# Six PSUM tiles in place of three double ones, gate and value evicted one by one, and mixer steps ranked higher

## The chip, the cores and the metric

The kernel runs on one core of a Trainium2 chip. The metric is the device time of one execution in microseconds (us). The engines are named as in the profile: PE is TensorE's matmul stream and PEld its weight loads, DVE is VectorE, ACT is ScalarE, POOL is GpSimd, SP is SyncE, which issues the transfers.

## The reference

Two layers of a streaming encoder for 256 frames of width 1024, all in float32:

```python
for layer in range(2):
    x = half_ffn(x, ffn_norm[layer, 0], w1, w3, w2)      # x + 0.5 * (silu(h w1) * (h w3)) w2, h = rmsnorm(x)
    h = rmsnorm(x, mix_norm[layer])
    x = x + (mixer_gla_rglru(h) if layer == 0 else mixer_hgrn2(h))
    x = half_ffn(x, ffn_norm[layer, 1], w1, w3, w2)
    gate = sigmoid(rmsnorm(x, ple_norm[layer]) @ ple_gate[layer])
    x = x + gate * (p[layer] @ ple_proj[layer])
return rmsnorm(x, final_norm)
```

The feed-forwards are 1024 to 2816 and back. The first mixer has four gated linear-attention heads and a gated linear recurrence (RG-LRU) with a short convolution, the second has eight heads of a gated recurrence with 128 by 128 states. Each head output goes through a norm of its own, is multiplied with silu of a gate, and then through an output projection.

## The kernel before, in words

Activations lie with the features on the partitions: x is 8 tiles of 128 features by 256 frames. The weights are one stream of 128 by 128 blocks in the order of their use. A transfer (`load`, L394) brings 16 blocks into one of three `raw` buffers. For exactness each weight is split in two parts, for eight blocks at a time: ACT copies them to the short form `wh` (L415) and DVE subtracts that to get the rest `wl` (L416); six buffers of each go round. Activations are split the same way. In the feed-forwards a block (`blk`, L453 and L454, in its last step L450 and L451) is one matmul of `wh` with both parts of the activation (512 columns, one whole PSUM bank) and one of `wl` with the first part (256 columns). In the mixers and the embedding a block (`blk3`, L437 to L439) is three matmuls of 256 columns into half a bank; where the frames are to lie on the partitions, `aproj` (L598 to L600) swaps the operands.

Products are summed in PSUM. There are eight banks. Two, `sgl`, are tiles of their own and serve small products. Six are halves of three tiles `duo` (L317 to L341): `bank()` hands them out in turn, and `bank2()` hands out the two halves of one `duo` together.

A feed-forward (`ffn`) has 22 lifts and 8 down projections. A lift makes the gate in one half of a `duo` and the value in the other; when both are complete, `lift` copies the `wl` halves of both by one ACT instruction of 512 columns (L613), adds them by one DVE instruction (L614), multiplies the gate with the norm's factor (L615), takes silu (L616), multiplies (L617) and splits the result (L618, L619). A down projection uses one bank and is evicted by a copy (L645) and an addition (L646), followed by a scaling and the addition to x. The norm's factor comes from a sum of squares by way of a square root on ACT (L563) and a reciprocal on DVE (L565).

In the mixers, `pairs` makes two products in one bank and `gated2` evicts them (L751); the head outputs `po` get a bank each (L956, L1095), and `Heads.norm` reads it twice: first for the squares (L720), whose mean goes through a root (L730) and two reciprocals (L733), and then for the scaling (L734). `gated` multiplies with the gate (L739) and `split` makes the two parts (L744, L745). In mixer1 the forget gates go through softplus straight from PSUM (L1020).

The order of the work on each engine is written by a planner (`Plan`). Every step is added with its engine, an estimated cost and what it reads and writes. The main matmuls keep the order of the stream. Every other step gets a due time, the latest at which PE would not have to wait for it, and at each moment an engine takes the ready step with the earliest due time. The instructions are then written out in that order, and each engine works through its list in turn. Waits between engines are set by the framework, by the tiles that instructions share. The planner itself follows parts of tiles (`Cell`), so it does not know of waits that come from a shared tile.

Of the kernel before, what the change touches and what calls it, by code (L numbers as in the profile page):

```python
# [13 lines left out]
P = 128  # L14
# [33 lines left out]
class Op:  # L48
    __slots__ = ("eng", "cost", "emit", "deps", "succ", "main", "due", "tab", "port", "left", "ready", "start",
                 "end", "seq", "first", "tag", "lag")  # L50

# [8 lines left out]
MARGIN = 350  # L60
HOLD = 25000


# [4 lines left out]
class Plan:  # L68
    def __init__(self):
        self.ops, self.now = [], 0.0  # L70
        self.phase = None

    def add(self, eng, cost, emit, r=(), w=(), main=False, tab=None, port=False, first=None, tag="", lag=0):
        o = Op()
        o.eng, o.cost, o.emit, o.main, o.tab, o.port, o.first, o.tag, o.lag = eng, cost, emit, main, tab, port, first, tag, lag
        o.deps, o.succ, o.seq = {}, [], len(self.ops)
        r, w = list(r), list(w)
# [27 lines left out]
    def order(self):  # L105
# [7 lines left out]
        for o in reversed(ops):  # L113
            d = o.due if o.eng == "PE" and o.main else last + 2000 - o.cost
            for s in o.succ:
                d = min(d, s.due - s.deps[o] - o.cost)
            o.due = d if o.first is None else o.first
        engines = ("PE", "DVE", "ACT", "POOL", "SP", "NONE")
        free = dict.fromkeys(engines, 0.0)
# [5 lines left out]
        for o in ops:  # L125
            if not o.left:
                heapq.heappush(wait[o.eng], (0.0, o.seq, o))

        def at(e):
# [5 lines left out]
        while len(out) < len(ops):  # L135
# [61 lines left out]
            if o.port:  # L197
                port = o.end
            out.append(o)
            for y in o.succ:  # L200
                y.left -= 1
                y.ready = max(y.ready, o.end + y.deps[o])
                if not y.left:
                    t = y.ready
                    if y.eng == "PE" and not y.main:
                        t += MARGIN
                    heapq.heappush(wait[y.eng], (t, y.seq, y))
        self.out = out
# [29 lines left out]
def kernel(  # L238
# [61 lines left out]

    def dve(n, emit, r, w, port=True, tag=""):
        return plan.add("DVE", 150 + 1.05 * n, emit, r, w, port=port, tag=tag)

# [12 lines left out]

    duo = [pp.tile([P, 2, 2, T], F32, name=f"duo{k}", tag=f"duo{k}") for k in range(3)]  # L317
    sgl = [pp.tile([P, 2, T], F32, name=f"sgl{k}", tag=f"sgl{k}") for k in range(2)]
    banks = []
    for k in range(6):  # L320
        b = Buf()
        b.t = duo[k // 2][:, k % 2]
        banks.append(b)
    sbanks = []
    for k in range(2):
        b = Buf()
        b.t = sgl[k]
        sbanks.append(b)
    sbank = Ring(sbanks)
    bi = [0]  # L330

    def bank():
        bi[0] += 1
        return banks[(bi[0] - 1) % 6]

    def bank2():

        bi[0] += bi[0] % 2
        k = bi[0] % 6
        bi[0] += 2  # L340
        return banks[k], banks[k + 1], duo[k // 2]  # L341

# [54 lines left out]
    def sub(i):  # L397
        if i in subs:
            return subs[i]
        ri, k = divmod(i, RB // SB)  # L400
        if ri not in raws:
            if ri < 4:
                load(ri, 0, 2)
                load(ri, 2, 4)
            else:
                load(ri, 0, 4)
        rb, h, l = raws[ri], wh_ring(), wl_ring()
        n = 2 if i < fine else 1
        for e in range(n):
            w = SB * P // n  # L410
            d = slice(e * w, (e + 1) * w)
            s = slice(k * SB * P + e * w, k * SB * P + (e + 1) * w)
            q = rb(2 * k + e) if n == 2 else rb(2 * k, 2 * k + 1)
            keys = (e,) if n == 2 else (0, 1)
            act(w, lambda d=d, s=s: A.copy(h.t[:, d], rb.t[:, s]), q, h(*keys), tag="wh")  # L415
            dve(w, lambda d=d, s=s: V.tensor_tensor(l.t[:, d], rb.t[:, s], h.t[:, d].bitcast(F32), ALU.subtract),  # L416
                q + h(*keys), l(*keys), tag="wl")
        subs[i] = (h, l)
        return subs[i]
# [185 lines left out]
    def ffn(nm, h, nxt, side=None):  # L605
        ph = Phase(f"f{nm}")
        t_ring, s_ring, lo_ring = ph.ring(2, [P, 2, T], "t"), ph.ring(2, [P, T], "s"), ph.ring(2, [P, 2, T], "lo")
        u2 = [ph.buf([P, 2, T], f"u2_{k}", F32R) for k in range(NF)]

        def lift(f, ba, bb, d):  # L610
            lo, t, s = lo_ring(), t_ring(), s_ring()
            ab = ba() + bb()
            act(2 * T, lambda: A.copy(lo.t, d[:, :, 1]), ab, lo(), tag="lo")  # L613
            dve(2 * T, lambda: V.tensor_add(t.t, d[:, :, 0], lo.t), ab + lo(), t(0, 1), port=False, tag="merge")  # L614
            dve(T, lambda: V.tensor_mul(t.t[:, 0], t.t[:, 0], h.r()), t(0) + h.rb(), t(0), tag="tr")  # L615
            act(T, lambda: A.activation(s.t, t.t[:, 0], AF.Silu), t(0), s(), tab="silu", tag="silu")  # L616
            dve(T, lambda: V.tensor_mul(t.t[:, 1], t.t[:, 1], s.t), t(1) + s(), t(1), tag="tb")  # L617
            act(T, lambda: A.copy(u2[f].t[:, 0], t.t[:, 1]), t(1), u2[f]("h"), tag="uh")  # L618
            dve(T, lambda: V.tensor_tensor(u2[f].t[:, 1], t.t[:, 1], u2[f].t[:, 0].bitcast(F32), ALU.subtract),  # L619
                t(1) + u2[f]("h"), u2[f](), tag="ul")  # L620

        wide = [bank2() for _ in range(2)]
        for c in range(NC):
# [7 lines left out]
        for f in range(2, NF):  # L631
            ba, bb, d = bank2()
            for b in (ba, bb):
                for c in range(NC):
                    m, mb = h.chunk(c)
                    blk(b.t, b(), m, mb, c == 0, c == NC - 1)
            lift(f, ba, bb, d)
        if side is not None:
            side(ph)
        def down(j):  # L640
            b = bank()
            for f in range(NF):
                blk(b.t, b(), lambda f=f: u2[f].t, u2[f]("h", 0), f == 0, f == NF - 1)
            lo, t = lo_ring(), pt_ring()
            act(T, lambda: A.copy(lo.t[:, 0], b.t[:, 1]), b(), lo(), tag="lo")  # L645
            dve(T, lambda: V.tensor_add(t.t, b.t[:, 0], lo.t[:, 0]), b() + lo(), t(), port=False, tag="merge")  # L646
            dve(T, lambda: V.scalar_tensor_tensor(t.t, t.t, 0.5, h.r(), op0=ALU.mult, op1=ALU.mult), t() + h.rb(), t(),
# [146 lines left out]
    def mixer0(nm, h, nxt):  # L794
# [153 lines left out]
        for e in range(2):  # L948
            b = bank()
            rows = slice(e * 64, e * 64 + 64)  # L950
# [48 lines left out]
    def mixer1(nm, h, nxt):  # L999
# [10 lines left out]
        def half(hh):  # L1010
# [77 lines left out]
            for k in range(2):  # L1088
                b = bank()

# [27 lines left out]
    for layer, mixer in enumerate((mixer0, mixer1)):  # L1118
        hm = Normed(f"m{layer}", ("mix", layer * NC), cols=True)
        ffn(f"{layer}0", h, hm, decay_terms if layer == 0 else lower_bound_terms)  # L1120
        hf = Normed(f"f{layer}1", ("ffn", (2 * layer + 1) * NC))
        mixer(f"{layer}", hm, hf)
        hl = Normed(f"p{layer}", ("ple", layer * NC))
        embed(layer)
# [182 lines left out]
```

## Time and profile before

| | us |
|---|---|
| median of 3 runs | 1104.5 |
| lowest, highest | 1101.99, 1104.57 |
| the profiled execution, its own time | 1102.52 |
| its span, first to last instruction | 1100.7 |
| PE busy (share of the span) | 1055.4 (96%) |
| DVE busy | 797.1 (72%) |
| ACT busy | 656.5 (60%) |
| POOL busy | 13.0 (1%) |

One execution was recorded. The busy time of PE counts a matmul until its modelled end; matmuls overlap, and a new one can begin while the one before it is still draining. "Idle before" is the time in which an engine did nothing ahead of an instruction, with what released it. The mean granted clock of PE is 0.994 of full speed. The stages follow each other on one time line: the first feed-forward ends near 202 us, mixer0 near 302, the second feed-forward near 494, the first embedding near 523, the third feed-forward near 718, mixer1 near 863, the last feed-forward near 1055, and then come the last embedding and the final norm.

### The profile page before, as it was taken

The numbers are of one execution on the slowest core, as the hardware profiler recorded it, in microseconds if no ns is written. First come the engines' busy times: TensorE is split into PE (matmuls) and PEld (weight loads), VectorE is DVE, ScalarE is ACT, GpSimd is POOL, SyncE is SP. The second block draws the span as 40 slices with busy tenths as digits, with TensorE's granted clock in tenths as the row PEclk, the third lists the DMA queues.
The fourth block names the chain that finished last, engine by engine and source line by source line (L and its number), as shares of the span: only waits on it lengthen the run. The fifth ranks groups of instructions, "written<-read, shape, count | busy, mean of one in ns | idle before, by whom it ended". The sixth has DMA issues, their size and how long they took to land.

```text
span 1100.7 us, 16250 instructions
## 1 busy us (share of the span) xinstructions
PE 1055.4 (96%) x6452; PEld 931.0 (85%) x6452; DVE 797.1 (72%) x1173; ACT 656.5 (60%) x973; POOL 13.0 (1%) x22
## 2 busy tenths in 40 slices
PE   8999999999999999999999999999998999999995
PEld 7888878889988888889888888789898888887885
DVE  7877766668887776668887776686868877775673
ACT  6666544576666565446765554495856655664452
POOL 4000000000000000000000000000000000000000
PEclk9999999999999999999999999999999999999998
DMA  7656654542555555544555554454433555555421
GB/s 269 230 196 229 211 191 153 178 152 78 203 206 183 181 187 187 180 164 150 196 191 188 182 193 165 159 186 153 149 120 118 187 182 180 182 188 188 158 75 38
DMA packets 28776, 190.14 MB, mean 173 GB/s; under 512 B 3323, under 2 KB 4380, under 8 KB 6684
## 3 DMA queue, kind: packets, MB, share of 16 engines
q1 hardware_dynamic: 28268, 188.53, 49.6%
q8 instruction: 50, 0.82, 0.3%
q10 hardware_dynamic: 432, 0.58, 0.2%
q14 instruction: 26, 0.21, 0.1%
HBM read 188.05 MB, written 1.05 MB: 172 GB/s over the span
## 4 chain that ended last, share of the span: by engine, by line
PE 92%; DVE 3%; ACT 2%; issue 1%; POOL 1%; DMA 0%; SPq 0%; DVEq 0%; ACTq 0%; POOLq 0%
PE duo L453 40%; PE duo L454 20%; PE duo L437 6%; PE duo L438 5%; PE duo L439 5%; PE duo L451 4%; PE duo L450 2%; PE duo L598 2%; PE duo L600 1%; PE duo L599 1%; DVE hsd_m L733 1%; PE duo L1095 1%; DVE pt L646 1%; ACT lo_f L645 1%; DMA xs<-in_xT_dram 0%
## 5 line engine op out<-in xcount | busy, mean ns | idle before, releaser
L416 DVE TENSOR_TENSOR wl<-raw,wh 128x1024 fp32r<-128x1024 f32 (+1 forms) x357 | 431.4, 1213 | 133.1 <-ACT wh L415 132.6
L415 ACT CAST wh<-raw 128x1024 fp32r<-128x1024 f32 (+1 forms) x357 | 368.9, 1038 | 197.7 <-PE duo L453 87.8
L453 PE MATMUL duo<-x,wh 128*128 128x512 f32 x1232 | 442.2, 398 | 3.4 <-DVE x L507 1.5
L454 PE MATMUL duo<-x,wl 128*128 128x256 f32 x1232 | 346.0, 281 | 1.6 <-DVE wl L416 1.6
L453 PEld LDWEIGHTS duo<-x,wh 128*128 128x128 f32 x1232 | 231.8, 188 | 53.0 <-ACT wh L415 2.2
L453 PE MATMUL duo<-u_f,wh 128*128 128x512 f32 x672 | 241.7, 398 | 17.7 <-DVE pt L646 9.4
L454 PEld LDWEIGHTS duo<-x,wl 128*128 128x128 f32 x1232 | 232.8, 189 | 9.5 <-DVE wl L416 2.2
L454 PE MATMUL duo<-u_f,wl 128*128 128x256 f32 x672 | 189.7, 282 | 0.0
L453 PEld LDWEIGHTS duo<-u_f,wh 128*128 128x128 f32 x672 | 126.1, 188 | 54.3 <-DVE pt L646 14.5
L437 PE MATMUL duo<-x,wh 128*128 128x256 f32 x496 | 143.6, 290 | 8.6 <-DVE gt L686 2.1
L438 PE MATMUL duo<-x,wh 128*128 128x256 f32 x496 | 141.1, 284 | 2.8 <-DVE x L745 2.8
L439 PE MATMUL duo<-x,wl 128*128 128x256 f32 x496 | 140.9, 284 | 0.0
L454 PEld LDWEIGHTS duo<-u_f,wl 128*128 128x128 f32 x672 | 126.3, 188 | 1.5
L613 ACT COPY lo_f<-duo 128x512 f32<-128x512 f32 x88 | 51.3, 587 | 119.3 <-PE duo L451 118.8
L437 PEld LDWEIGHTS duo<-x,wh 128*128 128x128 f32 x496 | 95.6, 193 | 12.9 <-DVE gt L686 2.9
L614 DVE TENSOR_TENSOR t_f<-duo,lo_f 128x512 f32<-128x512 f32 x88 | 60.5, 691 | 58.8 <-ACT lo_f L613 58.2
L438 PEld LDWEIGHTS duo<-x,wh 128*128 128x128 f32 x496 | 95.6, 193 | 3.4 <-DVE x L745 3.0
L439 PEld LDWEIGHTS duo<-x,wl 128*128 128x128 f32 x496 | 95.8, 193 | 0.0
L451 PE MATMUL duo<-x,wh 128*128 128x512 f32 x176 | 69.4, 398 | 0.0
L450 PE MATMUL duo<-x,wl 128*128 128x256 f32 x176 | 49.7, 282 | 0.0
L616 ACT ACTIVATE s_f<-t_f 128x256 f32<-128x256 f32 x88 | 36.4, 418 | 20.2 <-DVE t_f L615 20.0
L506 ACT ACTIVATE x<-xs,sml 128x256 fp32r<-128x256 f32 x64 | 31.6, 507 | 19.8 <-DVE xs L649 9.8
(210 smaller groups left out, 976.3 us busy)
## 6 DMA issues: line engine op xcount, KB each, us to landing
raw<-in_ws_dram SPq DMA_DIRECT2D x172, 1024.0 KB, 4.9
raw<-in_ws_dram SPq DMA_DIRECT2D x7, 512.0 KB, 8.5
xs<-in_xT_dram SPq DMA_DIRECT2D x3, 256.0 KB, 6.2
raw<-in_ws_dram SPq DMA_DIRECT2D x2, 256.0 KB, 4.7
praw<-in_pT_dram SPq DMA_DIRECT2D x1, 512.0 KB, 5.9
lb_D<-in_lbl_dram SPq DMA_DIRECT2D x1, 512.0 KB, 5.9
lb_A<-in_lbl_dram SPq DMA_DIRECT2D x1, 512.0 KB, 6.9
bd_m<-in_bdiag_dram SPq DMA_DIRECT2D x1, 512.0 KB, 3.6
```

What stands on the lines that cost most here:

```text
L415: act(w, lambda d=d, s=s: A.copy(h.t[:, d], rb.t[:, s]), q, h(*keys), tag="wh")
L416: dve(w, lambda d=d, s=s: V.tensor_tensor(l.t[:, d], rb.t[:, s], h.t[:, d].bitcast(F32), ALU.subtract), q + h(*keys), l(*keys), tag="wl")
L437: M.matmul(o, wh, mt[:, 0], start=first, stop=False)
L438: M.matmul(o, wh, mt[:, 1], start=False, stop=False)
L439: M.matmul(o, wl, mt[:, 0], start=False, stop=last)
L450: M.matmul(o[:, 0], wl, mt[:, 0], start=False, stop=False)
L451: M.matmul(o, wh, mt, start=first, stop=True)
L453: M.matmul(o, wh, mt, start=first, stop=False)
L454: M.matmul(o[:, 0], wl, mt[:, 0], start=False, stop=False)
L613: act(2 * T, lambda: A.copy(lo.t, d[:, :, 1]), ab, lo(), tag="lo")
L614: dve(2 * T, lambda: V.tensor_add(t.t, d[:, :, 0], lo.t), ab + lo(), t(0, 1), port=False, tag="merge")
L616: act(T, lambda: A.activation(s.t, t.t[:, 0], AF.Silu), t(0), s(), tab="silu", tag="silu")
```

## The change

- The three `duo` tiles and two `sgl` tiles become six tiles `bank` and two tiles `sbank` of one bank each. `bank2()` is gone.
- In `lift` the gate and the value each get a copy and an addition of 256 columns of their own (`merged`), and the gate goes on to silu before the value is read. The three rings behind it hold three tiles of 256 columns.
- In the mixers the stream of products uses banks 0 to 3 (`ring_mix`), and the head outputs banks 4 and 5 (`obank`). Elsewhere all six go round (`ring_all`).
- The due time of each step that is added in a mixer is moved 10 us ahead (`EARLY`), except for the weight conversions.
- While DVE is planned to do a long instruction that does not use the port shared with POOL (over 1.5 us, which means a reciprocal), the planner may hand one subtraction `wl` of 1024 columns that is ready to POOL, if it is not due for 3.6 us.

```diff
 HOLD = 25000
+ALT_NS = 2600
+EARLY = 10000
 
...
         self.ops, self.now = [], 0.0
-        self.phase = None
-
-    def add(self, eng, cost, emit, r=(), w=(), main=False, tab=None, port=False, first=None, tag="", lag=0):
+        self.early = 0
+
+    def add(self, eng, cost, emit, r=(), w=(), main=False, tab=None, port=False, first=None, tag="", lag=0, alt=None):
         o = Op()
+        o.alt = alt
         o.eng, o.cost, o.emit, o.main, o.tab, o.port, o.first, o.tag, o.lag = eng, cost, emit, main, tab, port, first, tag, lag
-        o.deps, o.succ, o.seq = {}, [], len(self.ops)
+        o.deps, o.succ, o.seq, o.early = {}, [], len(self.ops), self.early
         r, w = list(r), list(w)
...
             o.due = d if o.first is None else o.first
+        for o in ops:
+            o.due -= o.early
         engines = ("PE", "DVE", "ACT", "POOL", "SP", "NONE")
...
                 port = o.end
+            done(o)
+            if e == "DVE" and not o.port and o.cost > 1500 and free["POOL"] <= s0 and port <= s0:
+
+                fit = [y for y in ready[e] + wait[e] if y[2].alt and y[2].ready <= s0 + 300
+                       and y[2].due - s0 > ALT_NS + 1000]
+                if fit:
+                    x = min(fit, key=lambda y: y[2].due)
+                    for q in (ready[e], wait[e]):
+                        if x in q:
+                            q.remove(x)
+                            heapq.heapify(q)
+                    y = x[2]
+                    y.eng, y.emit = "POOL", y.alt
+                    y.start = max(s0, y.ready + 90)
+                    y.end = y.start + ALT_NS
+                    free["POOL"] = port = y.end
+                    y.end += 60
+                    done(y)
         self.out = out
...
 
-    def dve(n, emit, r, w, port=True, tag=""):
-        return plan.add("DVE", 150 + 1.05 * n, emit, r, w, port=port, tag=tag)
+    def dve(n, emit, r, w, port=True, tag="", alt=None):
+        return plan.add("DVE", 150 + 1.05 * n, emit, r, w, port=port, tag=tag, alt=alt)
 
...
 
-    duo = [pp.tile([P, 2, 2, T], F32, name=f"duo{k}", tag=f"duo{k}") for k in range(3)]
-    sgl = [pp.tile([P, 2, T], F32, name=f"sgl{k}", tag=f"sgl{k}") for k in range(2)]
-    banks = []
-    for k in range(6):
-        b = Buf()
-        b.t = duo[k // 2][:, k % 2]
-        banks.append(b)
-    sbanks = []
-    for k in range(2):
-        b = Buf()
-        b.t = sgl[k]
-        sbanks.append(b)
-    sbank = Ring(sbanks)
-    bi = [0]
+    banks = [common([P, 2, T], f"bank{k}", pool=pp) for k in range(6)]
+    ring_all, ring_mix, obank = Ring(banks), Ring(banks[:4]), Ring(banks[4:])
+    stream = [ring_all]
 
     def bank():
-        bi[0] += 1
-        return banks[(bi[0] - 1) % 6]
-
-    def bank2():
-
-        bi[0] += bi[0] % 2
-        k = bi[0] % 6
-        bi[0] += 2
-        return banks[k], banks[k + 1], duo[k // 2]
+        return stream[0]()
+
+    sbank = Ring([common([P, 2, T], f"sbank{k}", pool=pp) for k in range(2)])
 
...
         rb, h, l = raws[ri], wh_ring(), wl_ring()
+        early, plan.early = plan.early, 0
         n = 2 if i < fine else 1
...
             act(w, lambda d=d, s=s: A.copy(h.t[:, d], rb.t[:, s]), q, h(*keys), tag="wh")
-            dve(w, lambda d=d, s=s: V.tensor_tensor(l.t[:, d], rb.t[:, s], h.t[:, d].bitcast(F32), ALU.subtract),
-                q + h(*keys), l(*keys), tag="wl")
+
+            def low(E, d=d, s=s):
+                E.tensor_tensor(l.t[:, d], rb.t[:, s], h.t[:, d].bitcast(F32), ALU.subtract)
+
+            dve(w, lambda low=low: low(V), q + h(*keys), l(*keys), tag="wl", alt=n == 1 and (lambda low=low: low(G)))
+        plan.early = early
         subs[i] = (h, l)
...
         ph = Phase(f"f{nm}")
-        t_ring, s_ring, lo_ring = ph.ring(2, [P, 2, T], "t"), ph.ring(2, [P, T], "s"), ph.ring(2, [P, 2, T], "lo")
+        t_ring, s_ring, lo_ring = (ph.ring(3, [P, T], n) for n in ("t", "s", "lo"))
         u2 = [ph.buf([P, 2, T], f"u2_{k}", F32R) for k in range(NF)]
 
-        def lift(f, ba, bb, d):
-            lo, t, s = lo_ring(), t_ring(), s_ring()
-            ab = ba() + bb()
-            act(2 * T, lambda: A.copy(lo.t, d[:, :, 1]), ab, lo(), tag="lo")
-            dve(2 * T, lambda: V.tensor_add(t.t, d[:, :, 0], lo.t), ab + lo(), t(0, 1), port=False, tag="merge")
-            dve(T, lambda: V.tensor_mul(t.t[:, 0], t.t[:, 0], h.r()), t(0) + h.rb(), t(0), tag="tr")
-            act(T, lambda: A.activation(s.t, t.t[:, 0], AF.Silu), t(0), s(), tab="silu", tag="silu")
-            dve(T, lambda: V.tensor_mul(t.t[:, 1], t.t[:, 1], s.t), t(1) + s(), t(1), tag="tb")
-            act(T, lambda: A.copy(u2[f].t[:, 0], t.t[:, 1]), t(1), u2[f]("h"), tag="uh")
-            dve(T, lambda: V.tensor_tensor(u2[f].t[:, 1], t.t[:, 1], u2[f].t[:, 0].bitcast(F32), ALU.subtract),
-                t(1) + u2[f]("h"), u2[f](), tag="ul")
-
-        wide = [bank2() for _ in range(2)]
+        def merged(b, d):
+
+            lo = lo_ring()
+            act(T, lambda: A.copy(lo.t, b.t[:, 1]), b(), lo(), tag="lo")
+            dve(T, lambda: V.tensor_add(d.t, b.t[:, 0], lo.t), b() + lo(), d(), port=False, tag="merge")
+
+        def lift(f, ba, bb):
+            s, t = s_ring(), t_ring()
+            merged(ba, s)
+            dve(T, lambda: V.tensor_mul(s.t, s.t, h.r()), s() + h.rb(), s(), tag="tr")
+            act(T, lambda: A.activation(s.t, s.t, AF.Silu), s(), s(), tab="silu", tag="silu")
+            merged(bb, t)
+            dve(T, lambda: V.tensor_mul(t.t, t.t, s.t), t() + s(), t(), tag="tb")
+            split(lambda: t.t, t(), u2[f])
+
+        wide = [[bank() for _ in range(2)] for _ in range(2)]
         for c in range(NC):
...
         for f in range(2, NF):
-            ba, bb, d = bank2()
-            for b in (ba, bb):
+            ab = [bank() for _ in range(2)]
+            for b in ab:
                 for c in range(NC):
                     m, mb = h.chunk(c)
                     blk(b.t, b(), m, mb, c == 0, c == NC - 1)
-            lift(f, ba, bb, d)
+            lift(f, *ab)
         if side is not None:
             side(ph)
         def down(j):
             b = bank()
             for f in range(NF):
                 blk(b.t, b(), lambda f=f: u2[f].t, u2[f]("h", 0), f == 0, f == NF - 1)
-            lo, t = lo_ring(), pt_ring()
-            act(T, lambda: A.copy(lo.t[:, 0], b.t[:, 1]), b(), lo(), tag="lo")
-            dve(T, lambda: V.tensor_add(t.t, b.t[:, 0], lo.t[:, 0]), b() + lo(), t(), port=False, tag="merge")
+            t = pt_ring()
+            merged(b, t)
             dve(T, lambda: V.scalar_tensor_tensor(t.t, t.t, 0.5, h.r(), op0=ALU.mult, op1=ALU.mult), t() + h.rb(), t(),
...
         for e in range(2):
-            b = bank()
+            b = obank()
             rows = slice(e * 64, e * 64 + 64)
...
             for k in range(2):
-                b = bank()
+                b = obank()
 
...
         hf = Normed(f"f{layer}1", ("ffn", (2 * layer + 1) * NC))
+        stream[0], plan.early = ring_mix, EARLY
         mixer(f"{layer}", hm, hf)
+        stream[0], plan.early = ring_all, 0
         hl = Normed(f"p{layer}", ("ple", layer * NC))
```

## Rows read from the trace of the kernel before

**Rows 1.** The chain that ended last, shares of the span by engine.

```profile
PE 92%; DVE 3%; ACT 2%; issue 1%; POOL 1%; DMA 0%; SPq 0%; DVEq 0%; ACTq 0%; POOLq 0%
```

**Rows 2.** Groups of instructions: busy us, mean ns; idle before, releasers.

```profile
L453 PE MATMUL duo<-u_f,wh 128*128 128x512 f32 x672 | 241.7, 398 | 17.7 <-DVE pt L646 9.4 <-ACT lo_f L645 8.3
...
L437 PE MATMUL duo<-x,wh 128*128 128x256 f32 x496 | 143.6, 290 | 8.6 <-DVE gt L686 2.1 <-DVE xs L656 2.1 <-DVE qs_m L751 1.6
```

**Rows 3.** PE's waits: what it waited for, total us, times, longest us.

```profile
PE duo L453 <- DVE pt L646: 9.4, 16, 0.6
PE duo L453 <- ACT lo_f L645: 8.3, 16, 0.5
PE duo L438 <- DVE x L745: 2.8, 1, 2.8
PE duo L437 <- DVE gt L686: 2.1, 4, 0.5
...
PE duo L453 <- DVE t_f L614: 1.5, 1, 1.5
```

**Rows 4.** Timeline, first feed-forward, 141.5 to 144.7: start us, length us.

```profile
141.53 0.28 PE L450 MATMUL duo<-u_f,wl 128*128 128x256 f32 x1
141.65 0.40 PE L451 MATMUL duo<-u_f,wh 128*128 128x512 f32 x1
141.89 0.39 PE L453 MATMUL duo<-u_f,wh 128*128 128x512 f32 x1
142.12 0.28 PE L454 MATMUL duo<-u_f,wl 128*128 128x256 f32 x1
...
142.50 0.37 ACT L645 COPY lo_f<-duo 128x256 f32<-128x256 f32 x1 [1.58 <-PE duo L454]
142.92 0.50 PE L453 MATMUL duo<-u_f,wh 128*128 128x512 f32 x1 [0.52 <-ACT lo_f L645]
...
143.65 0.42 DVE L646 TENSOR_TENSOR pt<-duo,lo_f 128x256 f32<-128x256 f32 x1 [1.47 <-PE duo L454]
...
144.12 0.50 PE L453 MATMUL duo<-u_f,wh 128*128 128x512 f32 x1 [0.59 <-DVE pt L646]
...
144.58 0.40 PE L453 MATMUL duo<-u_f,wh 128*128 128x512 f32 x1
```

**Rows 5.** Groups of instructions, shapes apart: the evictions of the feed-forwards.

```profile
L614 DVE TENSOR_TENSOR t_f<-duo,lo_f 128x512 f32<-128x512 f32 x88 | 60.5, 691 | 58.8 <-ACT lo_f L613 58.2
L613 ACT COPY lo_f<-duo 128x512 f32<-128x512 f32 x88 | 51.3, 587 | 119.3 <-PE duo L451 118.8 <-DVE t_f L614 0.5
...
L646 DVE TENSOR_TENSOR pt<-duo,lo_f 128x256 f32<-128x256 f32 x32 | 13.5, 423 | 27.0 <-PE duo L454 22.9 <-ACT lo_f L645 4.1
...
L645 ACT COPY lo_f<-duo 128x256 f32<-128x256 f32 x32 | 11.9, 372 | 25.8 <-PE duo L454 16.3 <-PE duo L451 9.5
```

**Rows 6.** Stretches: length, busy PE, PEld, DVE, ACT, POOL, granted clock, DMA, GB/s.

```profile
17.00:134.00 117.00, 117.00 (x666) 101.71 (x666) 94.12 (x138) 74.91 (x115) 0.60 (x2) 1.00 0.63 217
722.00:740.00 18.00, 18.00 (x85) 15.03 (x84) 15.96 (x20) 17.38 (x20) 0.00 (x0) 1.00 0.52 174
842.00:843.00 1.00, 1.00 (x7) 1.00 (x6) 1.00 (x3) 0.00 (x0) 0.00 (x0) 0.50 0.06 25
```

**Rows 7.** Timeline of ACT in mixer1, first half.

```profile
745.89 1.26 ACT L1020 ACTIVATE e_m<-duo,r 128x512 f32<-128x512 f32 x2
```

**Rows 8.** Timeline of DVE at the end of mixer1.

```profile
837.89 3.36 DVE L733 RECIPROCAL hsd_m<-hsd_m 128x256 f32<-128x256 f32 x2 [0.64 <-ACT hsd_m L730]
```

**Rows 9.** Waits of SP's transfer queue, longest.

```profile
SPq L394 <- DVE wl L416: 479.0, 78, 16.6
```

**Rows 10.** Groups of instructions, shapes apart: POOL, and DVE's narrow subtractions.

```profile
L416 DVE TENSOR_TENSOR wl<-raw,wh 128x512 fp32r<-128x512 f32 x10 | 9.3, 943 | 0.5 <-ACT wh L415 0.4
...
L527 POOL TENSOR_TENSOR acc<-acc,sq 128x256 f32<-128x256 f32 x7 | 6.9, 981 | 0.5
...
L520 POOL TENSOR_TENSOR acc<-xs 128x256 f32<-128x256 f32 x1 | 0.6, 613 | 2.8 <-DMA xs<-in_xT_dram 2.8
```

More of the change, by code (lines that the diff above doesn't have):

```diff
@@ L49 @@
     __slots__ = ("eng", "cost", "emit", "deps", "succ", "main", "due", "tab", "port", "left", "ready", "start",
-                 "end", "seq", "first", "tag", "lag")
+                 "end", "seq", "first", "tag", "lag", "early",
+                 "alt")
 LAT = {("PE", "DVE"): 190, ("PE", "ACT"): 220, ("ACT", "DVE"): 45, ("DVE", "ACT"): 60, ("DVE", "PE"): 100,
@@ L127, in order, with done @@
                 heapq.heappush(wait[o.eng], (0.0, o.seq, o))
+        def done(o):
+            out.append(o)
+            for y in o.succ:
+                y.left -= 1
+                y.ready = max(y.ready, o.end + y.deps[o])
+                if not y.left:
+                    t = y.ready
+                    if y.eng == "PE" and not y.main:
+                        t += MARGIN
+                    heapq.heappush(wait[y.eng], (t, y.seq, y))
         def at(e):
@@ L198, in order @@
                 port = o.end
[L199 to L207, printed above, removed]
+            done(o)
[15 more added lines that the diff above has]
+                    done(y)
         self.out = out
```

## The prediction

> **What bounds the kernel now.** I read the chain of waits first: 92% of what ended last is PE [rows 1], so only a change of PE's own work or of the stretches in which PE stands still can move the time. The change leaves every main matmul as it is; so I went to PE's idle time. In the groups of instructions two stand out: 17.7 us before the first matmuls of the down projections (L453 on u_f) and 8.6 us before those of the narrower blocks (L437 on x) [rows 2]. PE's list of waits splits the 17.7 us into 16 waits for the copy of L645 and 16 for the addition of L646, the two steps that evict a finished bank; the 8.6 us are 15 waits for an eviction too, four of them for the gate (L686) [rows 3].
>
> The timeline shows why an eviction holds PE up [rows 4]. The bank of one down projection is complete with the matmul at 141.65 (0.40 long). PE begins the next bank with blocks at 141.89 and near 142.2. The copy of the finished bank could start near 142.1, but starts at 142.50, named as waiting for the matmul of 142.12, which writes the *other* bank. PE's next matmul then waits for the copy (142.92), the addition (143.65) waits for that block's end, and the block after it (144.12) waits for the addition. Both banks are halves of one tile `duo`, and each instruction on a `duo` is held against those on its other half. That is a wait for nothing: no number is shared.
>
> **The change part by part.** All sums are against the profiled execution's own 1102.5 us (span 1100.7 and 1.8 around it); the median of the runs, 1104.5, lies 2.0 above it.
>
> *Each bank a tile of its own.* What one crossing costs: blocks that nothing holds follow each other in 0.36 (141.53 to 141.89), so the fourth from 141.89 on is due at 142.97; it comes at 144.58 [rows 4]. 1.61 are lost, of which 0.52 + 0.59 = 1.11 are idle by the record; the other 0.50, a quarter for each wait, are the modelled end of the matmul before and the longer first matmul after it. So a loss is its idle time plus 0.25 a wait: down projections 17.7 + 32 x 0.25 = 25.7, narrower blocks 8.6 + 15 x 0.25 = 12.4. They occur only where one half of a `duo` is read while its partner is written, and with six tiles that can't be. What is late next? The weights: but no wait for a conversion is listed in those places. The true release of a bank could also hold PE, but in the feed-forward six banks go round, so that at least 16 blocks (5.6 us) lie between a bank's end and its next use. I take all of it there: -38.1, and -25.7 as the weaker end, if the narrower ones turn into other waits.
>
> *Gate and value evicted one by one.* 88 copies of 512 columns (587 ns) become 176 of 256 (372), and 88 additions (691) become 176 (423) [rows 5]: 88 x 157 = 13.8 us more on ACT, 88 x 155 = 13.6 us more on DVE. In the first lift stage ACT is busy 74.9 and DVE 94.1 of 117 us while PE stands still for none of it [rows 6]; 20 lifts add 3.1 to each, so DVE goes from 80% to 83%. Cost on the path nothing, hidden by PE; if that cover fails, 13.6. The rings behind it now hold three feature tiles and not two. The one wait for an addition of L614 (1.5, or 1.8 with its quarter [rows 3]) falls at the start of the third feed-forward, where both slots of t wait for the norm's reciprocal: with a third slot I take it as gone, -1.8 (bounds 0 and -1.8).
> The Trainium skill (Perfetto Trace Analysis, Optimizing Scalar/DVE Operations) says that larger operations pay where the engine is saturated, and that smaller ones can pay where it is not but makes bubbles on others. By its first half this part would cost the 13.6, by its second nothing; the 80% is on the second side.
>
> *Head outputs in two banks, the mixers' stream in four.* Counting the banks handed out, mixer0 starts on banks that were emptied two projections earlier, but mixer1's second bank is that of the very last down projection. It comes free a copy and an addition, 0.37 + 0.42 [rows 4], and three handovers of about 0.1 after its last matmul, 1.1 in all, and PE has three wide matmuls, 0.7, to do before it: 0.4 lost, or 1.6 with a conversion of 1.2 in front; I take 0.5. Second, mixer1's queries now reuse the banks of its forget gates, and the second of these is read by softplus from 745.89 to 747.15 [rows 7] while PE wants it near 746.6; with the first bank's pair a loss of 0 to 2.2, taken as 0.8, since the same change moves softplus forward. That the head outputs leave the stream spares 0.3 of wait at most, which I leave out.
>
> *Mixer steps ranked 10 us higher.* They go ahead of the weight conversions on ACT and DVE. The place that can gain is the end of mixer1: PE waits 2.8 us for the low half of a head output (L745 [rows 3]), which stands on DVE behind two reciprocals, 3.36 [rows 8], and the clock is then granted at half, 0.50 at 842 [rows 6], which on some 15 matmuls of about 0.12 costs 1.4 more. With the quarter of its restart 4.4 in all. If the second head's root is taken before the silu table is loaded, the wait nearly vanishes. Against it, PE arrives there about 1.0 earlier, since one of the 15 waits (0.8 and its quarter) lies just before. Bounds -4.4 and +1.5; I take -1.0, that is -2.0 and the 1.0 given back. The loads inside the mixers carry the higher rank along on SP's queue, but SP spends its time (479 us in that one row) waiting for conversions to free a raw buffer [rows 9], and buffers come free in the order of the loads: nothing.
>
> *Conversions handed to POOL during reciprocals.* At most 20, for 12 head and 8 norm reciprocals. From the 256-column rows, one of 1024 columns is, as an estimate, 4 x 0.61 = 2.5 us with DVE still and 4 x 0.98 = 3.9 beside it [rows 10]; one is chosen only if it is not due for 3.6. DVE gives up 1.2 each time, off the path. So from a gain of 1 to a loss of 20 x (3.9 - 3.6) = 6; I take a loss of 0.5.
> The same page of the Trainium skill warns that the two engines share a port into SBUF, so that such a move might not help. At the kernel's start the trace agrees: 512-column subtractions beside POOL take 943 ns [rows 10], more than the 691 of an addition of that width [rows 5]. By that rule alone DVE gains nothing from the 20, and the sum stays.
>
> Sum: -25.7 - 12.4 - 1.8 - 1.0 + 0.5 + 0.8 + 0.5 = -39.1; 1102.5 - 39.1 = 1063.4, and I say 1063.
>
> **The rivals.**
> *The tail closes too:* mixer1's last wait goes in full and nothing new comes: 1102.5 - 25.7 - 12.4 - 1.8 - 4.4 = 1058. For it: ACT does a weight conversion there, just ahead of the silu table. Against: the chain from the head outputs to the output projection is as long as PE's work beside it.
> *The mixers give part back:* some of the 30 reuses in the ring of four become true waits, an eviction behind a pair of reciprocals coming 3.4 late. Four such are 14 us: 1077. For it: at the start of mixer1 DVE is busy 16.0 and ACT 17.4 of 18 us [rows 6]. Against: between a bank's end and its reuse lie 5 us or more of other PE work.
> *The lifts become bound by DVE:* the 13.6 come on the path, 1077. Against it the 83%.
> *It doesn't do what it says:* an eviction waits for PE's newest matmul whatever the tile; only the 1.8 and the 1.0 go: 1100. Against: the banks of `sgl`, tiles of their own, show no such wait in PE's list.
> *Slower, the conversions starve:* in the mixers a step with 10 us to spare now beats a conversion wanted at once. The place is each burst of mixer work, about six (recurrence and heads of mixer0, gates and heads of both halves of mixer1); the price up to 10 us of PE standing still. It decides from four full bursts, 40 us; six are 60: 1063 + 60 = 1123. For it: ACT's 17.4 of 18. Against: six buffers of eight blocks are 17 us of work ahead, more than the 10.
>
> **How the numbers follow.** Forecast 0.70; tail closes 0.10; mixers give back 0.10; lifts bound 0.04; doesn't do what it says 0.03; starved 0.03. The forecast's own range is 1058 to 1071, its small terms at their bounds. From 1055 to 1077 the range takes in the tail and the edge of the two at 1077, some 0.85 in all. Less than 0.3%, 3.3 us, can't be told from no change. At 1100 the fourth rival is a little under that line below the 1102.5, but over it below the median; I count its 0.03 as same, starvation's 0.03 as slower, the rest, 0.94, as faster.
>
> **What would show it.** In the changed trace: no waits of PE for L645's and L646's like before the down projections, blocks 0.36 apart across their banks; none of 0.5 to 0.8 before the narrow blocks; one of 0.4 to 1 at the start of mixer1; DVE near 83% in the first lift stage with PE full; 176 copies of 0.37 in the lifts; subtractions of 2.5 to 3.9 us on POOL; a gap no longer than before at the end of mixer1. I am wrong if PE waits for conversions inside the mixers, or still stops at every second down projection.

## The result, and the profile after

The changed kernel takes 1057.48 us (median of 4 runs, 1057.01 to 1058.71) against 1103.75 for the kernel before (now four runs; 1104.5 was the median of the first three): a ratio of 0.9585, with a 95% interval of 0.9568 to 0.9601. The profiled execution took 1057.13, 45.4 less than the one before. The page, and PE's waits (the longest, and the two inside mixer1):

```profile
span 1055.1 us, 16450 instructions
...
PE 1041.4 (99%) x6452; PEld 928.8 (88%) x6452; DVE 800.4 (76%) x1259; ACT 651.0 (62%) x1059; POOL 17.8 (2%) x24
...
PE 97%; DVE 1%; POOL 1%; DMA 1%; ACT 0%; issue 0%; SPq 0%; DVEq 0%; ACTq 0%; POOLq 0%
```

```profile
PE sbank L557 <- DVE sq L529: 1.7, 1, 1.7
PE bank L467 <- DVE x L521: 1.4, 2, 1.0
...
PE bank L612 <- DVE pt L628: 0.4, 1, 0.4
...
PE bank L452 <- DVE x L761: 0.3, 1, 0.3
```

The 16 + 16 waits of [rows 3] are gone, and so are the 15 before the narrower blocks; PE's share of the chain goes from 92% [rows 1] to 97%. What is left lies at the kernel's start and end, but for 0.4 at the start of mixer1 and 0.3 at its end. The crossing of [rows 4] now looks so (timeline of the same place: start, length):

```profile
141.61 0.40 PE L465 MATMUL bank<-u_f,wh 128*128 128x512 f32 x1
141.85 0.39 PE L467 MATMUL bank<-u_f,wh 128*128 128x512 f32 x1
142.08 0.28 PE L468 MATMUL bank<-u_f,wl 128*128 128x256 f32 x1
142.10 0.37 ACT L627 COPY lo_f<-bank 128x256 f32<-128x256 f32 x1 [1.23 <-PE bank L465]
...
142.20 0.39 PE L467 MATMUL bank<-u_f,wh 128*128 128x512 f32 x1
...
142.51 0.42 DVE L628 TENSOR_TENSOR pt<-bank,lo_f 128x256 f32<-128x256 f32 x1 [0.38 <-ACT lo_f L627]
...
142.55 0.40 PE L467 MATMUL bank<-u_f,wh 128*128 128x512 f32 x1
```

The copy starts 0.09 after its own bank's last matmul (141.61 + 0.40), names that matmul as its releaser, and PE's blocks follow at 0.35 through it. Copies and additions have become 256 columns wide, at nearly the length of the narrow ones in [rows 5], and the first lift stage answers to [rows 6]:

```profile
L627 ACT COPY lo_f<-bank 128x256 f32<-128x256 f32 x208 | 76.1, 368 | 46.8 <-PE bank L465 46.8
...
L628 DVE TENSOR_TENSOR t_f<-bank,lo_f 128x256 f32<-128x256 f32 x88 | 36.6, 417 | 2.9 <-ACT lo_f L627 2.9
L628 DVE TENSOR_TENSOR s_f<-bank,lo_f 128x256 f32<-128x256 f32 x88 | 36.6, 417 | 3.3 <-ACT lo_f L627 2.9
```

```profile
17.00:134.00 117.00, 117.00 (x666) 101.67 (x665) 95.57 (x161) 75.96 (x138) 0.56 (x2) 1.00 0.63 220
```

PE is full as before, DVE at 82% of it. Where the time went is best seen by stages, from one main matmul's start to the next stage's first (each worked out from the PE timeline of the profiled execution, in us; "down" is the first of four, "lift" the third of four, "embed" the sum of both embeddings, the second up to the first matmul of PE's last group, L1158):

| kernel | median | down | mixer0 | lift | mixer1 | embed |
|---|---|---|---|---|---|---|
| before | 1103.8 | 68.28 | 98.27 | 126.08 | 144.43 | 67.13 |
| after | 1057.5 | 61.82 | 95.30 | 124.33 | 134.60 | 62.37 |
| e1_order | 1077.2 | 61.82 | 96.52 | 127.30 | 146.66 | 65.77 |
| e2_tiles | 1067.9 | 61.82 | 95.48 | 124.33 | 144.33 | 62.36 |
| e3_noearly | 1066.4 | 61.82 | 95.30 | 124.33 | 143.58 | 62.37 |
| e4_allring | 1060.7 | 61.82 | 95.49 | 124.33 | 137.13 | 62.36 |
| e5_duo | 1167.7 | 68.12 | 100.96 | 140.32 | 140.36 | 67.11 |
| e6_noalt | 1060.7 | 61.81 | 95.31 | 124.33 | 138.32 | 62.66 |
| e7_twice | 1058.6 | 61.82 | 96.79 | 124.29 | 134.59 | 62.37 |
| e8_two | 1066.3 | 61.82 | 96.80 | 131.10 | 137.17 | 62.37 |
| e9_early5 | 1059.3 | 61.82 | 96.77 | 124.32 | 136.96 | 62.36 |
| e10_early20 | 1062.3 | 61.81 | 97.45 | 124.33 | 138.17 | 62.36 |
| e11_early40 | 1056.8 | 61.82 | 95.95 | 124.33 | 134.47 | 62.37 |
| e12_offset | 1056.7 | 61.82 | 98.30 | 124.32 | 133.86 | 62.37 |

PE waits for nothing in mixer0 of e7 to e10 and of e12; most of the 1.5 to 3.0 that it is longer there is a stretch in which the clock was granted at half (last section).

### The profile page after: what moved, and what is told of

It reads as the page before. It is cut to its first block, busy times and chain, and to the rows that moved or that the text cites. A ratio compares the mean times of both kernels' runs of the same rounds, so it can differ in the third digit from the quotient of the medians.

```text
span 1055.1 us, 16450 instructions
## 1 busy us (share of the span) xinstructions
PE 1041.4 (99%) x6452; PEld 928.8 (88%) x6452; DVE 800.4 (76%) x1259; ACT 651.0 (62%) x1059; POOL 17.8 (2%) x24
## 4 chain that ended last, share of the span: by engine, by line
PE 97%; DVE 1%; POOL 1%; DMA 1%; ACT 0%; issue 0%; SPq 0%; DVEq 0%; ACTq 0%; POOLq 0%
PE bank L467 41%; PE bank L468 21%; PE bank L451 6%; PE bank L452 6%; PE bank L453 6%; PE bank L465 5%; PE bank L464 2%; PE bank L612 2%; PE bank L614 2%; PE bank L613 2%; PE bank L1111 1%; DMA xs<-in_xT_dram 1%; PE sbank L1086 0%; POOL acc L541 0%; PE sbank L904 0%; PE sbank L1061 0%
## 5 line engine op out<-in xcount | busy, mean ns | idle before, releaser
L467 PE MATMUL bank<-x,wh 128*128 128x512 f32 x1232 | 442.2, 398 | 1.8 <-DVE x L521 1.4
L468 PE MATMUL bank<-x,wl 128*128 128x256 f32 x1232 | 346.0, 281 | 1.4 <-DVE wl L428 1.4
L467 PEld LDWEIGHTS bank<-x,wh 128*128 128x128 f32 x1232 | 231.8, 188 | 51.4 <-ACT wh L425 2.2
L468 PEld LDWEIGHTS bank<-x,wl 128*128 128x128 f32 x1232 | 232.7, 189 | 9.5 <-DVE wl L428 2.3
L467 PE MATMUL bank<-u_f,wh 128*128 128x512 f32 x672 | 237.2, 393 | 0.0
L468 PE MATMUL bank<-u_f,wl 128*128 128x256 f32 x672 | 189.8, 282 | 0.0
L467 PEld LDWEIGHTS bank<-u_f,wh 128*128 128x128 f32 x672 | 126.2, 188 | 27.7
L451 PE MATMUL bank<-x,wh 128*128 128x256 f32 x496 | 141.2, 285 | 0.0
L452 PE MATMUL bank<-x,wh 128*128 128x256 f32 x496 | 140.5, 283 | 0.3 <-DVE x L761 0.3
L453 PE MATMUL bank<-x,wl 128*128 128x256 f32 x496 | 140.3, 283 | 0.0
L468 PEld LDWEIGHTS bank<-u_f,wl 128*128 128x128 f32 x672 | 126.3, 188 | 1.6
L627 ACT COPY lo_f<-bank 128x256 f32<-128x256 f32 x208 | 76.1, 368 | 46.8 <-PE bank L465 46.8
L451 PEld LDWEIGHTS bank<-x,wh 128*128 128x128 f32 x496 | 95.1, 192 | 1.5 <-issue 0.8
L452 PEld LDWEIGHTS bank<-x,wh 128*128 128x128 f32 x496 | 95.1, 192 | 1.1 <-DVE x L761 0.5
L453 PEld LDWEIGHTS bank<-x,wl 128*128 128x128 f32 x496 | 95.1, 192 | 0.0
L465 PE MATMUL bank<-x,wh 128*128 128x512 f32 x176 | 69.5, 398 | 0.0
L464 PE MATMUL bank<-x,wl 128*128 128x256 f32 x176 | 49.7, 282 | 0.0
L464 PEld LDWEIGHTS bank<-x,wl 128*128 128x128 f32 x176 | 33.1, 188 | 8.0
L628 DVE TENSOR_TENSOR s_f<-bank,lo_f 128x256 f32<-128x256 f32 x88 | 36.6, 417 | 3.3 <-ACT lo_f L627 2.9
```

What stands on the lines that cost most here:

```text
L451: M.matmul(o, wh, mt[:, 0], start=first, stop=False)
L452: M.matmul(o, wh, mt[:, 1], start=False, stop=False)
L453: M.matmul(o, wl, mt[:, 0], start=False, stop=last)
L464: M.matmul(o[:, 0], wl, mt[:, 0], start=False, stop=False)
L465: M.matmul(o, wh, mt, start=first, stop=True)
L467: M.matmul(o, wh, mt, start=first, stop=False)
```

## The experiments

**e1_order: the shared tile, or the order of semaphores?**

```diff
-        return banks[(bi[0] - 1) % 6]
+        return banks[(0, 2, 4, 1, 3, 5)[(bi[0] - 1) % 6]]
```

> The kernel before with one line changed: single banks are handed out in the order 0, 2, 4, 1, 3, 5, so that two in a row never lie in the same double tile; tiles, evictions of 512 columns and ranks stay as before. Theory (PE stands because the other half of the same tile is being read): the crossings of the down projections go, 25.8 us, and most of the 12.4 before the narrower blocks; about 1066, up to 1075 if the head outputs, which are read late, now share a tile with other products. Rival (an eviction waits for PE's newest matmul whatever the tile): 1104, as before.

Measured 1077.2, ratio 0.9759 (0.9734 to 0.9784). All four down stages take 61.8: with the double tiles, the evictions and the ranks untouched, that one line brings the whole 25.8. So the waits came from two neighbours in one tile, and the rival is out. The total is 2 above the theory's end, since mixer1 gains nothing: a head output, read late, now holds the other half of a tile that is wanted, and the clock is granted at 0.50 for 10.2 us of mixer1 (3.4 in the kernel before). PE's waits:

```profile
PE duo L598 <- DVE ho_m L734: 3.2, 1, 3.2
...
PE duo L598 <- ACT e_m L1020: 1.4, 1, 1.4
```

**e2_tiles: the tiles and the single evictions alone** (`obank` goes in both of its places)

```diff
-EARLY = 10000
+EARLY = 0
...
-        stream[0], plan.early = ring_mix, EARLY
+        stream[0], plan.early = ring_all, EARLY
...
-            b = obank()
+            b = bank()
...
-            ... alt=n == 1 and (lambda low=low: low(G)))
+            ... alt=None)
```

> The changed kernel with only its first part: six tiles, evictions one by one and rings of three; no higher rank for mixer steps, all six banks go round everywhere, nothing handed to POOL. Theory (tiles make the crossings' 25.8 + 12.4 and the third slot 1.75; the end of mixer1 is closed by the ranks): about 1064, with PE still waiting 2 to 3 us for L761's result at the end of mixer1. Rival (the end of mixer1 was itself a result of the shared tiles, and ranks, head banks and POOL do nothing): 1057 to 1058.

Measured 1067.9, ratio 0.9677 (0.9663 to 0.9691): 4 above the theory, 10 above the rival. All stages but mixer1 are within 0.2 of the changed kernel's, the first lift (0.8 longer) aside; mixer1 takes 144.33, as long as before, though its crossings are gone. PE's waits show why:

```profile
PE bank L612 <- DVE ho_m L750: 5.7, 1, 5.7
PE bank L452 <- DVE x L761: 2.8, 1, 2.8
```

The first is a true one: the bank of a head output comes round again before its scaling has read it. The second is the old wait at mixer1's end. Together they are 8.5; behind the first the clock is granted at 0.50 for some 5 us more.

**e3_noearly: no higher rank**

```diff
-EARLY = 10000
+EARLY = 0
```

> The changed kernel without the 10 us by which mixer steps are moved ahead. Theory (the ranks close the end of mixer1): the wait before the output projection comes back, 3 to 5 us with the slow clock after it: 1061 to 1063. Rival (ranks do nothing): 1057.5, within 1.

Measured 1066.4, ratio 0.9667 (0.965 to 0.9683). The direction is the theory's, the size twice it: 9.0 in mixer1, where PE's waits sum to 7.7 and not 0.8, and the clock is granted at 0.50 for 6.8 us. The end has two waits now:

```profile
PE bank L452 <- DVE x L761: 3.6, 1, 3.6
PE bank L451 <- ACT x L760: 2.6, 1, 2.6
```

**e4_allring: no banks of their own for the head outputs** (`obank` goes in both of its places)

```diff
-        stream[0], plan.early = ring_mix, EARLY
+        stream[0], plan.early = ring_all, EARLY
...
-            b = obank()
+            b = bank()
```

> The changed kernel without banks of their own for the head outputs: all six go round everywhere, ranks stay. Theory (the split of the banks is nearly neutral): the 0.6 at the start of mixer1 goes, and where a head output's bank comes round again 0.3 to 0.7 comes back: 1057 to 1058. Rival (the mixers' gain needs the head banks, because a head output holds its bank until its reciprocals are done): 3 to 8 us more, 1060 to 1065.

Measured 1060.7, ratio 0.9613 (0.9599 to 0.9627): 3.2 more, the rival's size but not its cause. No wait for a head output comes back, and the one at mixer1's start is gone, as the theory had it; the wait for L761 at mixer1's end is 2.75 again.

**e5_duo: the changed kernel on three double tiles**

```diff
-    banks = [common([P, 2, T], f"bank{k}", pool=pp) for k in range(6)]
+    duo = [pp.tile([P, 2, 2, T], F32, name=f"duo{k}", tag=f"duo{k}") for k in range(3)]
+    banks = [Buf() for _ in range(6)]
+    for k in range(6):
+        banks[k].t = duo[k // 2][:, k % 2]
```

> The changed kernel with its six banks laid back into three double tiles; evictions one by one, ranks, head banks and POOL stay. Theory (shared tiles): the crossings come back, 25.8 + about 12, and each lift gets one too, since the gate is now read while the value is written into the other half: up to 88 x 1.6 = 141 more, so between 1095 and 1236, with PE waiting for L627 and L628. Rival (the single evictions and not the tiles made the gain): 1057 to 1062.

Measured 1167.7, ratio 1.0579 (1.0564 to 1.0595), 110 more than the changed kernel. The down stages are back at 68.1 (the third at 69.5), and the lifts, in which PE waited for no eviction before, lose 15 to 21 each: the gate's eviction now meets the value's matmuls in the other half. Of the 92 waits for a copy 76 lie in the lifts and 16 in the down projections, as do the 16 for L631's pt (PE's waits):

```profile
PE duo L470 <- ACT lo_f L630: 46.9, 92, 0.8
PE duo L470 <- DVE pt L631: 9.4, 16, 0.6
PE duo L470 <- DVE s_f L631: 5.9, 10, 0.6
```

A lift loses 0.7 to 1.0 and not 1.6, as most of them wait only once. Single evictions without single tiles are worse than the kernel before.

**e6_noalt: nothing handed to POOL**

```diff
-            ... alt=n == 1 and (lambda low=low: low(G)))
+            ... alt=None)
```

> The changed kernel with no subtraction handed to POOL (two are in it). Theory (they lie off the path): 1057.5, within 0.5. Rival (they relieve DVE in mixer1's tightest place): 1 to 3 us more.

Measured 1060.7, ratio 0.9605 (0.9589 to 0.9621): 3.2 more, the rival's size but again not its cause: only two subtractions lay on POOL, at 769 and 772 us in the middle of mixer1, where PE waits for nothing in either kernel. The 2.76 wait for L761 is back, 40 us later.

**e7_twice: is the work of the evictions hidden?**

```diff
             merged(ba, s)
+            merged(ba, s)
...
             merged(bb, t)
+            merged(bb, t)
```

> The changed kernel with both evictions of each lift done twice (the second time with the same result): per lift 2 x 0.37 more on ACT and 2 x 0.42 on DVE, which takes DVE from about 4.6 to 5.4 of the 5.65 us that PE needs for a lift (96%). Theory (PE hides them as long as DVE is below PE): 0 to 5 us more, 1057 to 1063, so that the doubled instructions of the change cost nothing. Rival (they come on the path): 88 x 0.85 = 75 us more at most, 1132.

Measured 1058.6, ratio 0.9587 (0.9573 to 0.9601), not to be told from the changed kernel. The first lift stage:

```profile
17.00:134.00 117.00, 117.00 (x666) 101.66 (x665) 101.99 (x191) 87.59 (x176) 1.68 (x2) 1.00 0.61 217
```

DVE and ACT are busy for 6.4 and 11.6 more in these 117 us, DVE for 87% of them and not the 96% expected, and PE does the same 666 matmuls. So the 13.8 and 13.6 that the change itself adds cost nothing.

**e8_two: rings of two**

```diff
-        t_ring, s_ring, lo_ring = (ph.ring(3, [P, T], n) for n in ("t", "s", "lo"))
+        t_ring, s_ring, lo_ring = (ph.ring(2, [P, T], n) for n in ("t", "s", "lo"))
```

> The changed kernel with rings of two feature tiles behind the lifts in place of three. Theory (the third slot removed the one wait at the start of the third feed-forward): 1.75 more, 1059. Rival (that wait went for another reason): 1057.5.

Measured 1066.3, ratio 0.9663 (0.9648 to 0.9677): 6.8 in the third lift stage, where PE waits 4.0 for a bank until the norm's reciprocal has freed a slot, and 2.6 in mixer1, the wait for L761 once more. The cause is the theory's; the size is not. The statistics of that norm end later in this order (the reciprocal starts 25.6 us into the stage, as in the changed kernel; before the change 22.8), and behind the wait the clock was granted at half for some 5.6 us, which makes up the other 2.8 (the wait, then a stretch behind it):

```profile
PE bank L467 <- DVE s_f L628: 4.0, 1, 4.0
```

```profile
542.00:546.00 4.00, 4.00 (x15) 3.41 (x14) 2.77 (x9) 1.70 (x5) 0.00 (x0) 0.50 0.37 156
```

**e9_early5, e10_early20, e11_early40: how much rank?**

```diff
-EARLY = 10000
+EARLY = 5000       # e9; 20000 in e10, 40000 in e11
```

> The changed kernel with mixer steps moved ahead by 5 us in place of 10. Theory (it is the place of mixer steps before the weight conversions that closes the end of mixer1, and more lead closes it further): between none (1066.4) and 10 us (1057.5), 1058 to 1063, with part of the wait at the end of mixer1. Rival (10 us was a lucky order of one moment, and the lead itself does little): anywhere from 1057 to 1067, not in order with the lead.

> The changed kernel with mixer steps moved ahead by 20 us. Six buffers of converted weights hold 17 us of PE's work. Theory of starvation (the fifth rival of the prediction, price up to the lead less the 17 us for each of about six bursts): PE waits for wl or wh in the mixers, 0 to 18 us more, 1057 to 1076. Rival (bursts of mixer work are too short to use up the lead): 1057.5, within 1.

> The changed kernel with mixer steps moved ahead by 40 us, so that in a mixer they go first whatever their need. Theory of starvation: waits for wl or wh of several us in both mixers, 1065 to 1120. Rival (bursts too short, ACT and DVE have room): 1057 to 1060.

Measured 1059.3, 1062.3 and 1056.8 (ratios 0.96, 0.9587 to 0.9614; 0.9615, 0.9602 to 0.9629; 0.9576, 0.9563 to 0.9589). No rank is much worse (e3); above that the time doesn't follow the lead. None of the three shows a wait for a conversion in a mixer, so starvation did not come even at 40 us. I take it that a step ranked early still waits for its inputs and the conversions run in those gaps; that was not tried by itself. The runs with 5 and 20 have the 2.8 wait for L761, those with 10 and 40 have 0.3.

What flips it shows in the timelines of ACT and DVE at mixer1's end. First the changed kernel, then e9:

```profile
803.90 0.67 ACT L746 ACTIVATE hsd_m<-sbank,eps_t 128x512 f32<-128x512 f32 x1
804.59 1.28 ACT L1119 ACT_TABLE_LOAD   x1
805.89 1.06 ACT L1119 ACTIVATE gs_m<-gs_m 128x1024 f32<-128x1024 f32 x1
...
807.59 1.75 DVE L749 RECIPROCAL hsd_m<-hsd_m 128x256 f32<-128x256 f32 x1
809.25 0.36 DVE L761 TENSOR_TENSOR x<-ho_m,x 128x256 fp32r<-128x256 f32 x1
```

```profile
805.63 1.28 ACT L1119 ACT_TABLE_LOAD   x1
806.93 1.06 ACT L1119 ACTIVATE gs_m<-gs_m 128x1024 f32<-128x1024 f32 x1
808.01 1.28 ACT L746 ACT_TABLE_LOAD   x1
809.31 0.69 ACT L746 ACTIVATE hsd_m<-sbank,eps_t 128x512 f32<-128x512 f32 x1
...
810.03 3.36 DVE L749 RECIPROCAL hsd_m<-hsd_m 128x256 f32<-128x256 f32 x2 [0.65 <-ACT hsd_m L746]
813.31 0.36 DVE L761 TENSOR_TENSOR x<-ho_m,x 128x256 fp32r<-128x256 f32 x1
```

In the changed kernel the second head's root (L746) comes before the silu table is loaded; in e9 silu goes first, and a table is loaded back for the root, which comes 5.4 later on the time line (1.7 of that is mixer1 starting later; 3.7 within the stage). Its two reciprocals then stand on DVE in front of the low half (L761) that PE wants, which comes 2.4 later within the stage. All of e4, e6, e8, e9 and e10 have this order, with a table loaded back, and a wait of 2.75 or 2.76 there; in e7, e11 and e12, as in the changed kernel, the root comes first and the wait is 0.3. So the 2.4 to 3.7 that each of the five loses in mixer1 are not the price of the part that it takes away, but of this one order of two steps. In e8 and e9 the clock stayed at 1.00 behind the wait; in e6 and e10, which lose most, it was granted at 0.50 for 3.4 us (in e4 too, which has no wait at mixer1's start). Which of the planner's comparisons turns the order was not followed.

**e12_offset: a version for the start of mixer1**

```diff
+        ring_mix.i += 2 * layer
         stream[0], plan.early = ring_mix, EARLY
```

> The changed kernel with the mixers' ring of four moved on by two banks before mixer1, so that it begins on banks 2 and 3 and not on the bank of the last down projection. Theory (the 0.4 us wait of PE for L628 at mixer1's start, 0.58 in all, is that bank's true release): 0.6 less, 1057 at most, and no such wait. Rival (the new order of the banks shifts the planner's choices at the end of mixer1, where 0.3 us of wait are left): 1 to 4 us more.

Measured 1056.7, ratio 0.9578 (0.9565 to 0.9591): mixer1 is 0.74 shorter and the wait for L628 gone, as expected; in the profiled execution mixer0 is 3.0 longer, by the clock (last section). Like e11, it is the fastest by its median, but neither can be told from the changed kernel by its interval.

## Why the prediction was right

Forecast 1063 with 1055 to 1077, faster with 0.94; measured 1057.5. By stages, of the 39.1 forecast and the 45.2 found up to PE's last group of matmuls:

- *Down projections:* 25.7 forecast, 4 x 6.46 = 25.8 found. The sum "idle time plus a quarter a wait" held, and e1 shows that its cause is the shared tile.
- *Single evictions:* forecast free under the cover of PE; found so, with DVE at 82% for the 83% said (e7). The second half of what the prediction cites from the Trainium skill (Perfetto Trace Analysis, Optimizing Scalar/DVE Operations), that smaller operations can pay where an engine is not saturated but makes bubbles on others, agrees so far: the smaller ones cost nothing. That they bring something no run shows, and on shared tiles they cost 110 (e5).
- *Third slot:* 1.8 forecast, 1.75 found; e8 shows that without it 6.8 would be lost, 4.0 of it a wait.
- *Narrower blocks outside mixer1:* of the 15 waits six lie in the embeddings, 4.8 found, and four in mixer0 (0.8, 0.2 and two of 0.5 idle): 3.0 found. Idle plus a quarter gives 4.8 and 3.0.
- *Start of mixer1:* 0.5 forecast, 0.58 found, and e12 takes it away. The 0.8 for softplus in the queries' bank did not come.
- *POOL:* at most 20 were counted, two came; the loss of 0.5 was none. One takes 2.4 us, a little under the 2.5 for DVE at rest:

```profile
L428 POOL TENSOR_TENSOR wl<-raw,wh 128x1024 fp32r<-128x1024 f32 x2 | 4.8, 2405 | 572.5 <-PE bank L614 571.5 <-ACT wh L425 1.1
```

- *Mixer1:* here lies nearly all of the difference. Forecast -4.3 (five crossings of 4.6, -1.0 for the ranks, +0.5 and +0.8), found -9.8. The mis-sized term is that of *Mixer steps ranked 10 us higher*, "I take -1.0". The wait at the end went from 2.8 to 0.3, the way that step named (the root before the silu table), the stretch at half clock behind it went too, and nothing was given back: the rival "the tail closes too", 1058, is what came. In all, PE's waits in mixer1 sum to 7.3 before and 0.8 after. 1.1 of that were four waits of 0.2 before the sums of the head norms, which stood in no term of the forecast, and the 0.3 for a head output that it left out (PE's waits before the change):

```profile
PE sgl L727 <- DVE hsp_m L722: 0.4, 2, 0.2
PE sgl L726 <- ACT hsp_m L721: 0.4, 2, 0.2
PE duo L598 <- DVE ho_m L734: 0.3, 1, 0.3
```

And the ranks are worth more than that end: without them mixer1 is 9.0 longer (e3), and with the tiles alone its crossings only make room for a true wait of 5.7 for a head output's bank (e2). "I take all of it there" was right for the other stages, but in mixer1 the crossings' gain is had only with the ranks. That the end closes is in part luck: with a lead of 5 or 20 in place of 10 the root comes after the silu table, and the time is 1059.3 or 1062.3.

The rival that was to make it slower, starving conversions, did not appear at four times the lead (e11). A true wait for a head output's bank, as in "the mixers give part back", came only without the ranks and the head banks (e2). That the change would not do what it says is refuted by e1 and e5 from both sides: e1 parts neighbours and keeps the double tiles, e5 keeps the changed kernel's order of the banks and only puts them into double tiles again.

## What to carry to other kernels

Where a matmul waits for the eviction of a bank that it doesn't write, look at what the two share: in this kernel two products in one tile were held against each other though no number was common, and handing out the banks in another order (one line, 26 us here) shows it before anything is rebuilt. Make evictions smaller only together with the tiles (e5: 110 us worse), and ask of each wait that goes which true one stands behind it (e2). In an order made by a planner, taking a part out also moves other steps: compare where the time is lost, not only the totals, before the part gets the credit.

## What the runs showed of the hardware

PE's clock was granted at half in mixer0 of e12 with no idle time before it. The same place (length, busy PE, PEld, DVE, ACT and POOL with the instructions of each, then the granted clock, DMA and GB/s) in the changed kernel, then in e12:

```profile
244.00:246.00 2.00, 2.00 (x21) 1.93 (x20) 1.59 (x3) 1.93 (x4) 0.00 (x0) 1.00 0.72 217
246.00:248.00 2.00, 2.00 (x19) 2.00 (x19) 1.56 (x3) 0.79 (x1) 0.00 (x0) 1.00 0.73 307
```

```profile
244.00:246.00 2.00, 2.00 (x19) 1.96 (x17) 1.53 (x3) 1.99 (x4) 0.00 (x0) 0.78 0.84 225
246.00:248.00 2.00, 2.00 (x10) 1.92 (x10) 1.62 (x3) 0.00 (x0) 0.00 (x0) 0.50 0.71 299
248.00:250.00 2.00, 2.00 (x11) 2.00 (x11) 0.10 (x1) 1.17 (x2) 0.00 (x0) 0.50 0.00 0
```

In both, PE had just done the 32 matmuls of 64 columns of the head outputs (from 242.3 on) and was busy throughout. In one its clock stayed at 2.4 GHz, in the other it was at 1.2 GHz from 245.1 to 252.0, and PE did about half as many matmuls. That is the 3.0 by which mixer0 is longer in e12. In e7, e8, e9 and e10 the clock was at half in the same place for 3.4 us, which cost some 1.5.

And a wait of 2.8 at mixer1's end was followed by half the clock in the kernel before [rows 6], in e4, e6 and e10, but not in e8, nor in e9 (1.00 from 813 to 817). What decides it no run here shows. It differs between executions of one kernel too: two runs of e10 took 1059.65 with a mean granted clock of 0.996 and 0.997, the other three 1062.3 to 1062.5 with 0.992 and 0.993. So a difference of 1 to 3 us between two variants can lie in the clock alone: read the granted clock of a stage before its time is put down to a change.
